# A decoder layer's RWKV recurrence spawned behind its key projection, with its low-rank factors loaded at the unit's start

## The chip, the cores and the metric

The kernel runs on one core of a Trainium2 chip. The metric is the time of one execution on the device in microseconds; the time before is the median of three runs. A profiled execution beside them gives the trace from which all rows below come.

## The reference, cut to what matters

One layer with 1024 tokens of width 2048, all in float32. One input projection feeds two groups of heads: 16 RWKV-7 heads of 64 and 16 sliding-window attention heads of 64. Both are gated, and one output projection adds their result to the input.

```python
z = rms_norm(x, norm_w) @ w_in                       # 2048 -> 6528 columns
# RWKV half: z = z + (z_prev - z) * mu; r, k, v, g, wl, al = split(z)
decay = exp(-exp(-softplus(-(w0 + tanh(wl) @ w2)) - 0.5))
a  = sigmoid(a0 + al @ a2)
kk = l2norm(k * k_k);  k = k * (1 + (a - 1) * k_a)
# per token and head:
sa = S @ -kk_t;  S = S * decay_t + sa (kk_t * a_t)^T + v_t k_t^T;  o_t = S @ r_t
o  = layernorm(o) * lnx_w + lnx_b + sum(r * k * r_k) * v;  y_rwkv = o * silu(g)
# attention half: window 128, sinks, relative bias, RMS norm of q and k
out = x + concat(y_rwkv, y_att) @ w_out
```

## The kernel before, in words

**Tiling.** The tokens are taken in two halves of 512 (`hf`), the heads in eight pairs (`p`). A *unit* is one pair in one half. A projection tile (`ztile`, L325) gives 128 columns of `z` for the 512 tokens: 16 blocks of the contraction, each with three matmuls of 128x512 (L346 and L347 for the high part of the weight with the high and low parts of the activation, L351 for the low part of the weight), so 48 matmuls. ScalarE cuts each weight piece into a high part (L321), GpSimd subtracts to get the low part (L322); SP's queue loads the pieces (L335).

**A unit** (`unit`, L802) makes six projection tiles in order: key, receptance, value and gate of the RWKV pair, then query and gate of an attention pair. `shifted` (L357) mixes each of the first four with the token before (L360 to L363). The first unit of the second half has two tiles more (`att_kv`).

**The recurrence of a pair** is `rwkv` (L830). `rwkv_prep` loads the low-rank factors (L376), splits them (L378 to L383), squares the key (L387), makes decay and mixing factors from two low-rank products (`lora`, L389) and a head-wise sum (`headsum`, L558), with a reciprocal on VectorE (L404), and writes the chunk factors Gt (L428, L429) and F (L433, L434). L443 multiplies these in two batches, L446 to L449 mask the products. `solve` (L462) inverts a triangular matrix per chunk of 64 tokens: blocks of 16 on VectorE (L470, L471), sent through DRAM by six DMAs (L476, L478) and put together by small matmuls (L486 to L521). Then `rwkv_chain` walks over the eight chunks, each step a matmul L587, copies L590 and L592, matmuls L594 and L595, and an update of the state on VectorE, L598. `rwkv_post` copies the outputs (L608), normalises them, transposes (L625) and writes to DRAM (L630). The attention of the pair is `att` (L669), with softmax on ScalarE and VectorE (L696 to L718).

**What sets the order.** The work is written as Python generators with due times on a clock of their own, `clk`, in units close to microseconds; a projection tile counts 15.36, a unit 92.16. `yield t` hands control back until the clock of the loop `run` (L100) reaches `t`, and sets the due time of what follows through `at` (L92); a generator that yields a time that is already past is continued at once, with that earlier due time. The framework below orders each engine's instructions by due time among those that can go. A buffer, though, is asked for where the Python code makes the tile, so in the order in which the generators are run: a tag has a fixed number of buffers (L79: four of `t`, five of `ta` and `zt`; three PSUM banks of `m`), and a later request waits behind an earlier one of its tag.

`rwkv` counts its due times from `t0`, the unit's start: the square is due at 15.5, the receptance's use at 32, L443 at 57.2 and 62.4, the solve from 65 to 88.5, the chain from 91.5, the post step at 135 to 154. Before the change it is spawned behind the value tile, at 46.1 (L808). The tag `t` serves the preparation (L386, L397, L402, L411, L416, L538, L548) and the post step (L604, L616, L626). At the start of the second half `hprep` (L273) loads 16 blocks of the input with SP's queue (L254), transposes them on TensorE (L287) and splits them.

Of the kernel before, what the change touches and what calls it, by code (L numbers as in the profile page):

```python
# [19 lines left out]
P = 128  # L20
# [3 lines left out]
T = 512  # L24
# [40 lines left out]
def layer(tc, x, norm_w, w_in, w_out, mu_rwkv, w0, w2, a0, a2, k_k, k_a, r_k, lnx_w, lnx_b,  # L65
          q_norm_w, k_norm_w, sinks, rel_bias, cst, out, groups=range(NP), do_out=True, dbg=None):
    nc = tc.nc
# [7 lines left out]
    def sb(shape, tag, bufs=1, dt=F32):  # L75
        return pool.tile(list(shape), dt, name=tag, tag=tag, bufs=bufs)
# [4 lines left out]
    def tmp(tag="t"):  # L81
        return sb([P, T], tag, NT.get(tag, 1))
# [6 lines left out]
    MM, TILE = 0.32, 48 * 0.32  # L89
    clk = [20]  # L90

    def at(t):  # L92
        tc.cur_priority = 100000 + int(t * 1000)
# [3 lines left out]
    def spawn(gen, t=None):  # L97
        heapq.heappush(live, (now[0] if t is None else t, next(order), gen))
# [268 lines left out]
    def v3(t, n=T):  # L367
        return t.rearrange("p (c t) -> p c t", c=NC)

    def rwkv_prep(t0, hf, p, S, lor, zk, zr, zv):  # L370
        cp = slice(p * P, (p + 1) * P)
        yield t0 + 0.262
        wr = sb([P, 2, P], "k1", 2)
        for i, w in enumerate((w2, a2)):
            for hr in HR:
                nc.sync.dma_start(wr[hr, i, :], w[0, :, cp])  # L376
        wla = sb([P, 2, P], "wla", 1, F32R)
        A.copy(wla[:], wr[:])  # L378
        for i, hr in enumerate(HR):
            A.copy(whz[hr, i, :], wr[hr, i, :])  # L380
        for i in range(2):
            hr = HR[1 - i]
            G.tensor_tensor(wla[hr, i, :], wr[hr, i, :], wla[hr, i, :].bitcast(F32), ALU.subtract)  # L383
        yield t0 + 15.5

        sq = tmp()  # L386
# [29 lines left out]
        kmul = tmp()  # L416
        A.activation(kmul[:], pa[:], AF.Identity, bias=dv["cka"][:, p:p + 1], scale=dv["hka"][:, p:p + 1])
        V.scalar_tensor_tensor(pa[:], pa[:], 1.0, n2[:], ALU.add, ALU.mult)
        k3, r3 = v3(zk[:, 0:T]), v3(zr[:, 0:T])
        kP = Pi  # L420
        V.tensor_tensor(kP[:], zk[:, 0:T], Pi[:], ALU.mult)
        yield t0 + 32
        Gt = sb([P, NC, P], "Gt")
        F = [sb([P, 2, 4, P], "F", 3) for _ in range(2)]
        for i, hr in enumerate(HR):
# [36 lines left out]
        def solve():  # L462
# [7 lines left out]
                V.tensor_tensor(q, Xs[:, 0:j, j:j + 1].to_broadcast([64, j, n]), X[:, j:j + 1, j + 1:16].to_broadcast([64, j, n]), ALU.mult)  # L470
                V.tensor_tensor(X[:, 0:j, j + 1:16], X[:, 0:j, j + 1:16], q, ALU.add)  # L471
            A.copy(Xs[:], X)

            q = nc.gpsimd if hf == 0 and p == groups[-1] else nc.sync
            for x, h in halves:
                q.dma_start(x5.rearrange("i b c s t -> (i b c) s t")[:, h, h], Xs[x])  # L476
            for i, b, r, cb in quads:
# [57 lines left out]
                A.copy(BE[hr, c0:c0 + 4, hr], b[hr, :, hr])  # L535
        spawn(solve())
        yield t0 + 69.5
        vb = tmp()  # L538
        V.transpose(vb[:], zv[:])
        v4 = vb[:].rearrange("p (c k v) -> p c k v", c=NC, k=2)  # L540
# [128 lines left out]
    def att(t0, hf, p, Q, sq, gz):  # L669
# [8 lines left out]
        rq = rsqrt(ms[:], 8, "q")  # L678
        bia = sb([P, 2, P], "bia")
        nc.sync.dma_start(bia[:], bass.AP(tensor=bd.tensor, offset=bd[p:p + 1, 0:1].offset, ap=[[P - 1, P], [8 * P * P, 2], [1, P]]))  # L680
        yield t0 + 108.5
        pts = []
        Ls = [tmp("ta")[:].rearrange("p (b k) -> p b k", b=NB) for _ in range(2)]
        for b2 in range(2):
# [117 lines left out]
    def unit(hf, p, h, lor):  # L802

        S = {}
        zk = yield from shifted(h, 8 + p)
        zr = yield from shifted(h, p)
        zv = yield from shifted(h, 16 + p, True)
        spawn(rwkv(clk[0] - 3 * TILE, hf, p, S, lor, zk, zr, zv))  # L808
        zg = yield from shifted(h, 24 + p)

        def gate():
            S["sil"] = silu2(zg[:])
            yield

        spawn(gate(), clk[0] + 15)
        if hf and p == groups[0]:
            yield from att_kv(hf, h)

        z = yield from ztile(h, RWKV_COLS + p * 64, RWKV_COLS + 512 + p * 64)
        Q, sq = sb([P, 2, T], "Q", 1, F32R), tmp("zt")  # L820
        for i, hr in enumerate(HR):
            A.copy(Q[hr, i, :], z[hr])
            V.tensor_tensor(Q[HR[1 - i], i, :], z[hr], Q[hr, i, :].bitcast(F32), ALU.subtract)
        A.activation(sq[:], z[:], AF.Square)
        z = yield from ztile(h, RWKV_COLS + 1280 + p * 64, RWKV_COLS + 1792 + p * 64)
        gz = tmp("zt")
        A.copy(gz[:], z[:])
        spawn(att(clk[0] - 6 * TILE, hf, p, Q, sq, gz))
# [58 lines left out]
```

## Time and profile before

| | |
|---|---|
| median of three runs | 2066.15 us (2063.0 to 2070.83) |
| profiled execution | 2064.07 us |
| its span in the trace | 2062.3 us |
| TensorE busy | 1980.4 us, 96% |
| VectorE, ScalarE, GpSimd busy | 1197.1, 1040.2, 860.0 us |
| mean granted TensorE clock | 0.986 of full speed |

Busy time is the union of an engine's instructions; TensorE's matmuls are pipelined and their ends modelled, so the starts of consecutive ones tell more than their durations. "Idle before" is the time in which an engine stood still ahead of an instruction, with what ended it. L numbers are lines of the kernel before.

### The profile page before, as it was taken

The numbers are of one execution on the slowest core, as the hardware profiler recorded it, in microseconds if no ns is written. First come the engines' busy times: TensorE is split into PE (matmuls) and PEld (weight loads), VectorE is DVE, ScalarE is ACT, GpSimd is POOL, SyncE is SP. The second block draws the span as 40 slices with busy tenths as digits, with TensorE's granted clock in tenths as the row PEclk, the third lists the DMA queues.
The fourth block names the chain that finished last, engine by engine and source line by source line (L and its number), as shares of the span: only waits on it lengthen the run. The fifth ranks groups of instructions, "written<-read, shape, count | busy, mean of one in ns | idle before, by whom it ended". The sixth has DMA issues, their size and how long they took to land.

```text
span 2062.3 us, 36490 instructions
## 1 busy us (share of the span) xinstructions
PE 1980.4 (96%) x13152; PEld 1599.5 (78%) x13152; DVE 1197.1 (58%) x2776; ACT 1040.2 (50%) x2563; POOL 860.0 (42%) x746
## 2 busy tenths in 40 slices
PE   7999999999999999799999999999999989999999
PEld 5777777777778787577777777777777778988887
DVE  5747585857575857585666676758585864011001
ACT  5445555555655555555656464655555563223221
POOL 4543434434343434245353434343443433444443
PEclk9999999999999999899999999999999999999999
DMA  7332323232333325223232323232323263455443
GB/s 175 90 93 62 94 64 87 70 83 73 82 76 82 79 74 137 63 70 93 69 98 64 90 61 92 58 98 64 87 68 84 72 182 120 150 159 168 137 134 118
DMA packets 410341, 197.01 MB, mean 96 GB/s; under 512 B 214893, under 2 KB 379088, under 8 KB 410160
## 3 DMA queue, kind: packets, MB, share of 16 engines
q1 hardware_dynamic: 369216, 181.70, 31.9%
q10 hardware_dynamic: 40000, 11.67, 2.4%
q0 software_dynamic: 944, 1.31, 0.5%
q8 instruction: 103, 1.69, 0.3%
q14 instruction: 78, 0.64, 0.1%
HBM read 173.51 MB, written 21.10 MB: 94 GB/s over the span
## 4 chain that ended last, share of the span: by engine, by line
PE 37%; DVE 9%; issue 3%; POOL 2%; ACT 1%; DMA 1%; SPq 0%; ACTq 0%; POOLq 0%; DVEq 0%
PE z L351 6%; PE z L346 6%; PE z L347 6%; PE z L789 2%; PE m L791 2%; PE z L790 2%; PE m L789 2%; PE z L791 2%; PE m L790 2%; POOL wl L322 1%; PE o L791 1%; PE o L789 1%; PE o L790 1%; DVE t L404 1%; PE o L587 1%
## 5 line engine op out<-in xcount | busy, mean ns | idle before, releaser
L322 POOL TENSOR_TENSOR wl<-wr,wh 128x512 fp32r<-128x512 f32 x536 | 704.8, 1319 | 1000.0 <-ACT wh L321 494.9
L346 PE MATMUL z<-hh,wh 128*128 128x512 f32 x1632 | 668.6, 410 | 2.4 <-ACT wh L321 1.7
L347 PE MATMUL z<-hl,wh 128*128 128x512 f32 x1632 | 656.0, 402 | 0.6 <-DVE hl L263 0.6
L321 ACT CAST wh<-wr 128x512 fp32r<-128x512 f32 x536 | 331.1, 619 | 530.6 <-PE z L347 170.4
L351 PE MATMUL z<-hh,wl 128*128 128x512 f32 x1632 | 482.5, 406 | 0.0
L346 PEld LDWEIGHTS z<-hh,wh 128*128 128x128 f32 x1632 | 311.9, 191 | 73.5 <-ACT wh L321 4.0
L347 PEld LDWEIGHTS z<-hl,wh 128*128 128x128 f32 x1632 | 312.1, 191 | 62.6 <-DVE hl L263 1.5
L351 PEld LDWEIGHTS z<-hh,wl 128*128 128x128 f32 x1632 | 299.7, 190 | 63.8 <-issue 3.6
L354 DVE TENSOR_TENSOR z<-z,R 128x512 f32<-128x512 f32 x102 | 70.9, 695 | 117.9 <-PE z L351 115.4
L789 PE MATMUL z<-wh,hh 128*128 128x256 f32 (+1 forms) x352 | 112.1, 319 | 9.6 <-ACT hh L259 5.9
L590 ACT ACTIVATE s<-svu,pe 64x64 f32<-64x64 f32 x256 | 88.1, 344 | 52.0 <-DVE svu L598 48.6
L791 PE MATMUL z<-wh,hl 128*128 128x256 f32 (+1 forms) x352 | 111.1, 316 | 0.0
L790 PE MATMUL z<-wl,hh 128*128 128x256 f32 (+1 forms) x352 | 111.0, 315 | 0.0
L587 PEld LDWEIGHTS o<-svu,F 128*128 128x128 f32 x512 | 81.3, 190 | 27.4 <-DVE svu L598 16.8
L470 DVE TENSOR_TENSOR pr<-X,ch 64x14 f32<-64x14 f32 (+6 forms) x224 | 42.2, 188 | 98.3 <-ACT ch L465 91.4
L587 PE MATMUL o<-svu,F 128*128 128x64 f32 x512 | 83.9, 264 | 7.8 <-DVE svu L598 7.3
L797 DVE TENSOR_TENSOR ta<-z,ta 128x256 f32<-128x256 f32 (+1 forms) x22 | 9.9, 492 | 128.8 <-PE z L791 128.8
L598 DVE SCALAR_TENSOR_TENSOR svu<-ch,pe,s 64x64 f32<-64x64 f32 x224 | 63.1, 282 | 28.6 <-PE ch L594 23.8
L789 PEld LDWEIGHTS z<-wh,hh 128*128 128x128 f32 x352 | 67.0, 191 | 15.0 <-ACT hh L259 6.3
L797 DVE TENSOR_TENSOR ta<-m,ta 128x512 f32<-128x512 f32 x9 | 6.1, 690 | 124.8 <-PE m L791 124.8
L790 PEld LDWEIGHTS z<-wl,hh 128*128 128x128 f32 x352 | 67.1, 191 | 4.3
L791 PEld LDWEIGHTS z<-wh,hl 128*128 128x128 f32 x352 | 67.0, 190 | 4.3
(278 smaller groups left out, 3343.6 us busy)
## 6 DMA issues: line engine op xcount, KB each, us to landing
wr<-in_w_in SPq DMA_DIRECT2D x280, 256.0 KB, 2.9
wr<-in_w_in SPq DMA_DIRECT2D x256, 128.0 KB, 2.6
wr<-in_w_out SPq DMA_DIRECT2D x64, 256.0 KB, 2.9
wr<-in_w_out SPq DMA_DIRECT2D x128, 128.0 KB, 2.9
ta<-in_x SPq DMA_DIRECT2D x37, 256.0 KB, 5.2
zt<-yd SPq DMA_DIRECT2D x32, 256.0 KB, 3.5
out<-ta SPq DMA_DIRECT2D x24, 256.0 KB, 4.1
yd<-ta ACTq DMA_DIRECT2D x16, 256.0 KB, 2.6
```

Of the source, the lines that this page charges most:

```text
L321: A.copy(hi[:], raw)
L322: G.tensor_tensor(lo[:], raw, hi[:].bitcast(F32), ALU.subtract)
L346: PE.matmul(z[:], lhsT=wh, rhs=hh[kk][:], start=(kk == 0), stop=False)
L347: PE.matmul(z[:], lhsT=wh, rhs=hl[kk][:], start=False, stop=False)
L351: PE.matmul(z[:], lhsT=lo[:, k * P:(k + 1) * P], rhs=hh[kk][:], start=False, stop=(kk == KT - 1))
L354: V.tensor_tensor(z[:], z[:], R[:], ALU.mult)
L587: PE.matmul(O[:, c, i, :], lhsT=F[c // 4][:, i, c % 4, :], rhs=svu[:, i, c, :], start=c % 4 == 0 and i == 0, stop=False, skip_group_check= ...
L590: A.activation(s0[hr], svu[hr, i, c, :], AF.Copy, scale=pe[hr, c:c + 1])
L598: V.scalar_tensor_tensor(dst, ch[hr, i, :], pe[hr, c:c + 1], s0[hr], ALU.mult, ALU.add)
L789: PE.matmul(o, lhsT=yh[k][:, ts], rhs=wh, start=k == 0 and tt % n == 0, stop=False, skip_group_check=True)
L790: PE.matmul(o, lhsT=yh[k][:, ts], rhs=wl, start=False, stop=False, skip_group_check=True)
L791: PE.matmul(o, lhsT=yl[k][:, ts], rhs=wh, start=False, stop=k == KT - 1 and tt % n == n - 1, skip_group_check=True)
```

## The change

Five edits: the low-rank factors are loaded and split by a function of their own, called at the unit's start and due 8 before it (DMAs) and 2 behind it (splits), in a buffer of tag `t` where it was one of `k1`; `rwkv` is spawned behind the key tile, and gets the list in which receptance and value are put later; `rwkv_prep` takes them from the list where it uses them; the last pair's solve in the first half sends its six DMAs by SP's queue where it was GpSimd's; the attention asks for its logits buffers at 103.2 where it was 108.5.

```diff
--- before.py
+++ after.py
@@ -367,20 +367,27 @@
     def v3(t, n=T):
         return t.rearrange("p (c t) -> p c t", c=NC)
 
-    def rwkv_prep(t0, hf, p, S, lor, zk, zr, zv):
+    def low_rank(t0, p):
+
         cp = slice(p * P, (p + 1) * P)
-        yield t0 + 0.262
-        wr = sb([P, 2, P], "k1", 2)
+        at(t0 - 8)
+        wr = tmp()[:, 0:2 * P].rearrange("p (i c) -> p i c", i=2)
         for i, w in enumerate((w2, a2)):
             for hr in HR:
                 nc.sync.dma_start(wr[hr, i, :], w[0, :, cp])
+        at(t0 + 2)
         wla = sb([P, 2, P], "wla", 1, F32R)
-        A.copy(wla[:], wr[:])
+        A.copy(wla[:], wr)
         for i, hr in enumerate(HR):
             A.copy(whz[hr, i, :], wr[hr, i, :])
         for i in range(2):
             hr = HR[1 - i]
             G.tensor_tensor(wla[hr, i, :], wr[hr, i, :], wla[hr, i, :].bitcast(F32), ALU.subtract)
+        return wla
+
+    def rwkv_prep(t0, hf, p, S, lor, wla, zs):
+
+        zk = zs[0]
         yield t0 + 15.5
 
         sq = tmp()
@@ -416,10 +423,12 @@
         kmul = tmp()
         A.activation(kmul[:], pa[:], AF.Identity, bias=dv["cka"][:, p:p + 1], scale=dv["hka"][:, p:p + 1])
         V.scalar_tensor_tensor(pa[:], pa[:], 1.0, n2[:], ALU.add, ALU.mult)
-        k3, r3 = v3(zk[:, 0:T]), v3(zr[:, 0:T])
+        k3 = v3(zk[:, 0:T])
         kP = Pi
         V.tensor_tensor(kP[:], zk[:, 0:T], Pi[:], ALU.mult)
         yield t0 + 32
+        zr = zs[1]
+        r3 = v3(zr[:, 0:T])
         Gt = sb([P, NC, P], "Gt")
         F = [sb([P, 2, 4, P], "F", 3) for _ in range(2)]
         for i, hr in enumerate(HR):
@@ -470,8 +479,7 @@
                 V.tensor_tensor(q, Xs[:, 0:j, j:j + 1].to_broadcast([64, j, n]), X[:, j:j + 1, j + 1:16].to_broadcast([64, j, n]), ALU.mult)
                 V.tensor_tensor(X[:, 0:j, j + 1:16], X[:, 0:j, j + 1:16], q, ALU.add)
             A.copy(Xs[:], X)
-
-            q = nc.gpsimd if hf == 0 and p == groups[-1] else nc.sync
+            q = nc.sync
             for x, h in halves:
                 q.dma_start(x5.rearrange("i b c s t -> (i b c) s t")[:, h, h], Xs[x])
             for i, b, r, cb in quads:
@@ -535,6 +543,7 @@
                 A.copy(BE[hr, c0:c0 + 4, hr], b[hr, :, hr])
         spawn(solve())
         yield t0 + 69.5
+        zv = zs[2]
         vb = tmp()
         V.transpose(vb[:], zv[:])
         v4 = vb[:].rearrange("p (c k v) -> p c k v", c=NC, k=2)
@@ -678,7 +687,7 @@
         rq = rsqrt(ms[:], 8, "q")
         bia = sb([P, 2, P], "bia")
         nc.sync.dma_start(bia[:], bass.AP(tensor=bd.tensor, offset=bd[p:p + 1, 0:1].offset, ap=[[P - 1, P], [8 * P * P, 2], [1, P]]))
-        yield t0 + 108.5
+        yield t0 + 103.2
         pts = []
         Ls = [tmp("ta")[:].rearrange("p (b k) -> p b k", b=NB) for _ in range(2)]
         for b2 in range(2):
@@ -802,10 +811,11 @@
     def unit(hf, p, h, lor):
 
         S = {}
-        zk = yield from shifted(h, 8 + p)
-        zr = yield from shifted(h, p)
-        zv = yield from shifted(h, 16 + p, True)
-        spawn(rwkv(clk[0] - 3 * TILE, hf, p, S, lor, zk, zr, zv))
+        wla = low_rank(clk[0], p)
+        zs = [(yield from shifted(h, 8 + p))]
+        spawn(rwkv(clk[0] - TILE, hf, p, S, lor, wla, zs))
+        zs.append((yield from shifted(h, p)))
+        zs.append((yield from shifted(h, 16 + p, True)))
         zg = yield from shifted(h, 24 + p)
 
         def gate():
```

## Rows read from the trace of the kernel before

**Rows 1.** Page part 1: busy time of the engines over the span

```profile
PE 1980.4 (96%) x13152; PEld 1599.5 (78%) x13152; DVE 1197.1 (58%) x2776; ACT 1040.2 (50%) x2563; POOL 860.0 (42%) x746
```

**Rows 2.** Stretches: length, busy PE, PEld, DVE, ACT, POOL, clock, DMA share, GB/s

```profile
351.00:448.00 97.00, 94.58 (x667) 75.09 (x666) 65.47 (x160) 54.30 (x142) 39.70 (x35) 0.98 0.31 78
...
1515.00:1612.00 97.00, 94.51 (x674) 75.71 (x673) 66.28 (x158) 54.84 (x142) 39.94 (x35) 0.98 0.31 78
...
724.70:846.20 121.50, 105.87 (x888) 84.51 (x887) 69.78 (x168) 59.35 (x156) 45.29 (x42) 0.90 0.36 97
1177.90:1275.60 97.70, 95.25 (x677) 76.31 (x676) 66.76 (x158) 54.60 (x143) 39.96 (x35) 0.98 0.31 78
```

**Rows 3.** Timeline, TensorE, one unit: start, us, instruction, [idle before <-releaser]

```profile
1177.85 0.39 PE L346 MATMUL z<-hh,wh 128*128 128x512 f32 x1
1178.08 0.39 PE L347 MATMUL z<-hl,wh 128*128 128x512 f32 x1
...
1243.05 0.48 PE L443 MATMUL m<-F,Gt 64*128 64x128 f32 x2 [0.98 <-DVE F L434]
1243.99 1.17 PE L443 MATMUL m<-F,Gt 64*128 64x128 f32 x14 [0.46 <-DVE F L434]
...
1245.69 0.63 PE L346 MATMUL z<-hh,wh 128*128 128x512 f32 x1
...
1248.25 0.45 PE L346 MATMUL z<-hh,wh 128*128 128x512 f32 x1
```

**Rows 4.** Timeline, VectorE, the same unit

```profile
1194.89 0.75 DVE L361 SCALAR_TENSOR_TENSOR zt<-z,par,zt 128x511 f32<-128x511 f32 x1 [0.76 <-ACT zt L360]
...
1234.10 3.33 DVE L404 RECIPROCAL t<-t 128x512 f32<-128x512 f32 x1
...
1243.43 0.42 DVE L434 TENSOR_TENSOR F<-zt,Pc 64x256 f32<-64x256 f32 x1
```

**Rows 5.** Timeline, ScalarE, the same unit

```profile
1222.76 1.50 ACT L608 COPY t<-o 64x256 f32<-64x256 f32 x4
...
1226.96 0.71 ACT L387 ACTIVATE t<-zt,par 128x512 f32<-128x512 f32 x1
```

**Rows 6.** Timeline, TensorE, end of the first half

```profile
797.83 1.16 PE L443 MATMUL m<-F,Gt 64*128 64x128 f32 x16
...
822.40 0.71 PE L351 MATMUL z<-hh,wl 128*128 128x512 f32 x2
833.77 1.07 PE L486 MATMUL m<-k,Eab 32*32 32x32 f32 x64 [10.66 <-DVE k L482]
...
844.34 1.06 PE L287 MATMUL m<-cst,ta 128*128 128x128 f32 x4
...
846.17 0.50 PE L346 MATMUL z<-hh,wh 128*128 128x512 f32 x1
```

**Rows 7.** Waits: engine line <- releaser: us in total, times, longest

```profile
POOL wla L383 <- ACT wla L378: 57.4, 15, 15.7
...
PE m L443 <- DVE F L434: 18.9, 26, 1.0
...
PE o L587 <- DVE svu L598: 7.3, 14, 1.4
...
PE m L532 <- DVE F L449: 2.9, 7, 0.4
```

**Rows 8.** Timeline, solve's copy and return: ScalarE and VectorE, two units

```profile
822.89 0.36 ACT L472 COPY X<-ch 64x256 f32<-64x256 f32 x1
...
833.17 0.45 DVE L482 STREAM_TRANSPOSE k<-dg 128x256 f32<-128x256 f32 x1 [9.33 <-DMA dg<-xd]
...
1273.52 0.37 ACT L472 COPY X<-ch 64x256 f32<-64x256 f32 x1 [1.17 <-DVE ch L471]
...
1281.96 0.45 DVE L482 STREAM_TRANSPOSE k<-dg 128x256 f32<-128x256 f32 x1 [3.40 <-DMA dg<-xd]
```

**Rows 9.** Line L376, SP: issues, ns min/median/max, first and last start

```profile
L376 SPq DMA_DIRECT2D k<-in_w x32: 471/532/1524, 24.6 to 1583.9; - x32
L376 SPq DMA_DIRECT2D k<-in_a x32: 587/595/1702, 27.8 to 1585.2; - x32
```

**Rows 10.** Timeline, TensorE, the chain beside softmax in another unit

```profile
1304.61 0.43 PE L587 MATMUL o<-svu,F 128*128 128x64 f32 x2 [0.56 <-DVE svu L598]
```

## The prediction

> **What bounds the kernel now.** I read the page first: TensorE is busy for 1980.4 of 2062.3 us [rows 1]. That is an upper figure, because modelled matmul ends overlap, so I then read stretches of one unit (one head pair in one half). A usual unit lasts 97 to 98 us; in 1177.9 to 1275.6 TensorE is busy for 95 us, VectorE for 67, ScalarE for 55, GpSimd for 40 [rows 2]. Nothing but TensorE is full, so a unit gets shorter only where TensorE waits or runs slowly. TensorE takes its instructions in a fixed order: one matmul that waits holds the projections behind it.
>
> Then the timeline of such a unit. Its key tile starts on TensorE at 1177.85 [rows 3]. The key projection is ready in SBUF at about 1195.6, when the mixing step L361 ends [rows 4]. But the first step of the recurrence, the square at L387, runs only at 1226.96, 31 us later, on the heels of the copies L608 of the unit before (1222.76) [rows 5]. No data links the two. What links them is the tag `t`: the old order of the Python code asks for the post step's buffers (due 135 of the unit before, which is 42.8 of this one) ahead of the preparation's (due 15.5), since `rwkv` is spawned only behind the value tile (46.1). So the preparation stands behind a post step that is due 27 later.
>
> The late preparation then runs as one burst on VectorE: the reciprocal L404 at 1234.10, the last factor L434 that the first batch of L443 needs at 1243.43 [rows 4]. TensorE comes to L443 before that and waits 0.98 us and 0.46 us [rows 3]. [...]
>
> Last, the end of the first half: the unit there lasts 121.5 us at a mean clock of 0.90 [rows 2]. Projections run out at about 823.1, and TensorE sits idle for 10.66 us until L486 at 833.77, the solve of the last pair [rows 6]. The transposes L287 of the second half follow only at 844.34 [rows 6].
>
> **The change part by part.** The clock of the code runs 92.2 per unit, the chip 97: due times stretch by 1.05.
>
> (1) `rwkv` is spawned behind the key tile. No computing is added or removed; the preparation's requests for `t` and for the PSUM tag `m` move ahead of the post step's. The square can then start at 1195.6 instead of 1227, and the factors F are limited by the receptance tile (due 30.7, so about 34 us into the unit) and by VectorE's other work. From the unit's 34th us to L443's due time (57.2, so 60 us, 1238) there are 26 us, where the work from the reciprocal to the last needed factor now takes 9.8 us of VectorE (1234.10 to 1243.85, [rows 4]). So L443 finds its operands ready.
>
> Gain a: the waits of L443 for F, 18.9 us in 26 waits, that is 13 units [rows 7]. Gain b: the waits of L532 behind it, 2.9 us in 7 [rows 7]. Gain c: the slow stretches. Six of the seventeen 97 us stretches stand at 0.98 (the first and last in rows 2, outside the boundary); one costs 6 x (0.43 - 0.23) = 1.2 us, together 7.
>
> (2) At the boundary the second batch of L443 ran at 797.83, 73 us into its unit [rows 6]; with its operands ready it comes at its due time of 62.4, 65.5 us in, or 790.2. From there to L486 it took 35.9 us [rows 6], so L486 would be ready at 826.1. (3) That unit's solve moves its six DMAs from GpSimd's queue to SP's. On GpSimd's it took 10.3 us from the copy L472 (822.89) to L482 (833.17); a unit on SP's took 8.4 (1273.52 to 1281.96) [rows 8]. That is 1.9 more: ready at about 824.2, and the idle time falls from 10.7 to about 1. Gain d: 9.5 us. What would take it away: SP is also carrying the second half's input blocks then, and a DMA that waits there for its buffer holds all behind it. Bounds for the boundary: nothing, and the whole 23 us from 823.1 to the second half's first projection at 846.17 [rows 6]. I stay near the low middle, since the transposes' PSUM banks are still asked for behind the solve's.
>
> (4) The low-rank factors go into a `t` buffer at 8 before the unit, not a `k1` one. The same four DMAs stand in SP's queue, at medians of 0.53 and 0.60 us two each, 2.3 us a unit [rows 9]. They pass weight loads that are issued 17 ahead of use, which is the cover; without it each unit would lose up to 2.3 us, 37 in all. They hold a fourth of tag `t` for about 10 units of clock in which the post step due before is done and the preparation is not begun. The splits L378 to L383 move with them: GpSimd stands still at L383 for 57.4 us in 15 waits today, with its weight splits queued behind [rows 7], and no projection waits for that, so ending it earns nothing. I take 0. (5) The attention's logits buffers are asked for at 103.2, not 108.5, ahead of the preparation's first banks: no instruction differs; 0, with bounds of a few tenths either way that the terms below contain.
>
> (6) What is late next. The chain of the unit before (91.5 to 131, so 0 to 41 us into this unit) and the attention's softmax now share VectorE with the preparation. A chain step's update L598 that becomes ready behind the reciprocal waits up to 3.3 us (1234.10, [rows 4]), and TensorE waits at L587. Lower bound: a gain of 7.3, if the chain's dates, 5 apart, are kept so well that L587's present waits go [rows 7]. Upper bound: 3.3 us once a unit, 53, and a slow stretch behind each, 16 x 1.2 = 19. The nearest row is today's: chain beside softmax, L587 waits 0.56 us [rows 10]. I take that once more a unit, 9 us.
>
> [...]
>
> Sum: 18.9 + 2.9 + 7 + 9.5 - 9 = 29 us. The profiled execution took 2064.07 us, 1.8 beyond its span and 0.1% under the median of 2066.15; 2064 - 29 = 2035 by the one, 2037 by the other. I say 2036.
>
> **The rivals.** *The wait moves to the chain (slower).* Place: L587 and L594 on TensorE, behind L598 on VectorE. For it: in the first 41 us of a unit VectorE would hold chain, softmax, projection endings and the preparation at once, and the reciprocal alone lasts 3.33 us [rows 4]. Against: a unit leaves VectorE 31 us to spare [rows 2], and post step and factors have slack to slip behind the chain. Price: 53 + 19 = 72 lost against 38 gained, 2064 + 34 = 2098. It decides from 3.0 us a unit (38 + 10 over 16); below that it only eats the gain.
>
> *The wait keeps its size.* VectorE gets no further with F by L443 than now, or the chain takes as much as L443 gives back (1.8 us a unit). Only the boundary's 9.5 remains: about 2055, at the edge of what counts as faster. For it: the burst's work is the same, and the softmax stands in its way. Against: 31 us of head start.
>
> *It does not do what it says.* Something else than `t` holds L387, such as the bank order of `m`, and the square stays behind the post step: 2064. For it: the trace shows L387 behind L608 [rows 5], not why; it cannot tell a buffer from sheer order. Against: an operand that lies ready for 31 us, and ScalarE at only 55 of 98 us [rows 2].
>
> **How the numbers follow.** The forecast has 0.64, the wait that keeps its size 0.15, no effect 0.06, the slower rival 0.15. A measurement of this kernel tells about 0.5%, 10 us, from no change. Faster than that: the forecast and a fair part of the second case at its edge, less the forecast's own weak end: 0.66. Same: 0.19. Slower: 0.15. The forecast's own range is 2012 (no new wait, and the whole 23 us of the boundary: 2064 - 28.8 - 23) to 2053 (nothing at the boundary, and new waits twice as large: 2064 - 28.8 + 18). The range that should hold 8 in 10 goes from 2010 to 2072, which takes in the case with no effect and the mild part of the slower one.
>
> **What would show each step.** Right: in the changed kernel's timelines the square stands about 18 us after its unit's first key matmul, ahead of the post step's copies; "PE m L443 <- DVE F" is gone from the list of waits or under 4 us; no 0.98 in the stretches; L486 at the boundary waits under 3 us; the units last about 95. Wrong: the square still 49 us in; the wait of L443 unchanged; L587 or L594 with more than 1 us a unit; SP waiting ahead of the solve's DMAs at the boundary; or projections that wait for `wh` or `wl`, ScalarE's and GpSimd's splits come late behind the moved work.

## The result, and the profile after

The changed kernel takes 2038.06 us (median of 4 runs, 2035.18 to 2040.28), the kernel before, run beside it, 2065.92 (2063.0 to 2070.83): a ratio of 0.9862, 95% interval 0.9839 to 0.9885. The forecast was 2036. Line numbers from here on are those of the changed kernel: the square is L394 (was L387), the reciprocal L411 (L404), F L442 and L443 (L433, L434), the batches of L443 are now L452, the solve's first products L494 (L486), the chain's matmuls L596, L603, L604 (L587, L594, L595) and its update L607 (L598). Two single edits of the kernel before have numbers of their own, given where they are quoted.

The page, part 1, of the changed kernel, against [rows 1]:

```profile
span 2033.4 us, 36474 instructions
...
PE 1956.4 (96%) x13152; PEld 1588.8 (78%) x13152; DVE 1154.3 (57%) x2776; ACT 1038.9 (51%) x2563; POOL 855.4 (42%) x740
```

The span is 28.9 us shorter, TensorE's busy time 24.0. VectorE's fell by 42.8 with the same 2776 instructions, which no step of the prediction speaks of: added one by one, their durations are 31 us less, so some instructions got shorter. That is the first hint of what the experiments found.

The waits, against [rows 7] (us in total, times, longest):

```profile
PEld o L596 <- DVE svu L607: 30.9, 44, 2.5
...
PE o L596 <- DVE svu L607: 14.1, 19, 2.1
```

Among all of TensorE's waits none of L452 for F is left, where 18.9 us stood, and none of the transposes behind it (2.9). The chain's wait has doubled, from 7.3 us in 14 to 14.1 in 19. In all kernels of this document with the late spawn it is 4.7 to 7.3 us; in all with the early spawn and GpSimd's subtractions whole it is 14.1 to 28.7.

One unit, the pair that [rows 3 to 5] show, in the changed kernel: ScalarE, then VectorE, then TensorE (start, us, instruction). The unit's first key matmul is at 1162.9.

```profile
1180.88 0.73 ACT L394 ACTIVATE t<-zt,par 128x512 f32<-128x512 f32 x1
...
1210.96 1.50 ACT L617 COPY t<-o 64x256 f32<-64x256 f32 x4
```
```profile
1196.92 3.35 DVE L411 RECIPROCAL t<-t 128x512 f32<-128x512 f32 x1
...
1209.86 0.41 DVE L443 TENSOR_TENSOR F<-zt,Pc 64x256 f32<-64x256 f32 x1
```
```profile
1227.93 1.16 PE L452 MATMUL m<-F,Gt 64*128 64x128 f32 x16
...
1233.60 1.16 PE L452 MATMUL m<-F,Gt 64*128 64x128 f32 x16
1234.69 0.51 PE L346 MATMUL z<-hh,wh 128*128 128x512 f32 x1
```

The square stands 18.0 us into the unit (49 before) and 30 ahead of the post step's copies, where it used to follow them. The reciprocal is at 34.0 instead of 56. The factors are ready 15 us before L452, which runs without a bracket, that is without idle time before it.

Where the time went: the span cut at the first key matmul of units, in us. "End of half 1" is the last unit there with the first tile of half 2.

| stretch | before | after | difference |
|---|---|---|---|
| to the first key matmul, and the first unit | 140.6 | 141.5 | +0.9 |
| six usual units of half 1 | 584.1 | 563.2 | -20.9 |
| end of half 1 | 143.3 | 136.2 | -7.1 |
| first two units of half 2 | 210.6 | 225.7 | +15.1 |
| five usual units of half 2 | 490.3 | 473.7 | -16.6 |
| last unit and output projection | 493.3 | 493.2 | -0.1 |

So the usual units gained 37.5 us and the end of half 1 7.1, and the first two units of half 2 gave 15.1 back. Stretches (length, busy PE, PEld, DVE, ACT, POOL, clock, DMA share, GB/s) of the two units in the changed kernel, a usual unit, and the last of half 1:

```profile
840.90:971.20 130.30, 122.61 (x799) 96.84 (x799) 85.81 (x193) 71.25 (x176) 53.24 (x44) 0.99 0.28 73
971.20:1066.50 95.30, 88.29 (x436) 70.24 (x435) 62.54 (x141) 46.18 (x116) 40.95 (x35) 0.95 0.30 78
...
1162.90:1257.50 94.60, 92.86 (x678) 74.57 (x677) 63.65 (x158) 55.05 (x143) 40.05 (x35) 1.00 0.32 81
...
704.80:818.60 113.80, 102.65 (x887) 82.87 (x885) 65.64 (x168) 58.16 (x151) 40.74 (x34) 0.93 0.40 102
```

and of the same two in the kernel before:

```profile
868.10:994.90 126.80, 122.28 (x799) 95.94 (x799) 86.31 (x193) 71.41 (x176) 53.18 (x44) 1.00 0.29 76
994.90:1078.70 83.80, 83.73 (x436) 67.17 (x435) 59.35 (x141) 45.34 (x113) 39.73 (x33) 1.00 0.33 87
```

The second of them, with 436 matmuls where a usual unit has 678, was full: 83.73 of 83.80 us. Now it has 7 us of idle TensorE and a clock of 0.95. The usual unit shown no longer has 0.98, but 1.00.

### The profile page after: what moved, and what is told of

The parts are those of the page before. It is cut to its first block, busy times and chain, and to the rows that moved or that the text cites. A ratio compares the mean times of both kernels' runs of the same rounds, so it can differ in the third digit from the quotient of the medians.

```text
span 2033.4 us, 36474 instructions
## 1 busy us (share of the span) xinstructions
PE 1956.4 (96%) x13152; PEld 1588.8 (78%) x13152; DVE 1154.3 (57%) x2776; ACT 1038.9 (51%) x2563; POOL 855.4 (42%) x740
## 4 chain that ended last, share of the span: by engine, by line
PE 40%; DVE 8%; issue 3%; POOL 1%; ACT 1%; DMA 1%; ACTq 0%; SPq 0%; POOLq 0%; DVEq 0%
PE z L351 6%; PE z L346 6%; PE z L347 6%; PE z L798 2%; PE z L800 2%; PE z L799 2%; PE m L800 2%; PE m L798 2%; PE m L799 2%; POOL wl L322 1%; DVE ta L714 1%; PE o L800 1%; PE o L798 1%; PE o L799 1%; DVE t L411 1%
## 5 line engine op out<-in xcount | busy, mean ns | idle before, releaser
L322 POOL TENSOR_TENSOR wl<-wr,wh 128x512 fp32r<-128x512 f32 x536 | 704.4, 1318 | 952.2 <-ACT wh L321 506.7
L346 PE MATMUL z<-hh,wh 128*128 128x512 f32 x1632 | 661.4, 405 | 3.5 <-ACT hh L262 2.3
L351 PE MATMUL z<-hh,wl 128*128 128x512 f32 x1632 | 483.8, 406 | 0.0
L351 PEld LDWEIGHTS z<-hh,wl 128*128 128x128 f32 x1632 | 301.0, 190 | 65.1 <-issue 2.7
L596 PEld LDWEIGHTS o<-svu,F 128*128 128x128 f32 x512 | 81.5, 189 | 38.8 <-DVE svu L607 30.9
L596 PE MATMUL o<-svu,F 128*128 128x64 f32 x512 | 85.9, 264 | 15.0 <-DVE svu L607 14.1
L798 PEld LDWEIGHTS z<-wh,hh 128*128 128x128 f32 x352 | 67.1, 191 | 15.1 <-ACT hh L259 6.8
L607 DVE SCALAR_TENSOR_TENSOR svu<-ch,pe,s 64x64 f32<-64x64 f32 x224 | 62.9, 281 | 17.3 <-PE ch L603 11.1
```

Source lines behind the costliest of these rows:

```text
L322: G.tensor_tensor(lo[:], raw, hi[:].bitcast(F32), ALU.subtract)
L346: PE.matmul(z[:], lhsT=wh, rhs=hh[kk][:], start=(kk == 0), stop=False)
L351: PE.matmul(z[:], lhsT=lo[:, k * P:(k + 1) * P], rhs=hh[kk][:], start=False, stop=(kk == KT - 1))
L596: PE.matmul(O[:, c, i, :], lhsT=F[c // 4][:, i, c % 4, :], rhs=svu[:, i, c, :], start=c % 4 == 0 and i == 0, stop=False, skip_group_check= ...
L607: V.scalar_tensor_tensor(dst, ch[hr, i, :], pe[hr, c:c + 1], s0[hr], ALU.mult, ALU.add)
L798: PE.matmul(o, lhsT=yh[k][:, ts], rhs=wh, start=k == 0 and tt % n == 0, stop=False, skip_group_check=True)
```

## The experiments

Each is compared with the kernel before, run on the same chip. In the stretches, one profile differs from another by up to some 3 us where the kernels are alike: with GpSimd's queue restored for one pair (below), the six units that lie ahead of that pair, and which the edit doesn't touch, came out at 566.5 against 563.2. The chain's wait differs more: 14.1 us in the changed kernel, 15.4 to 21.3 in the four kernels below whose edits leave the chain alone (the queue, the late post step, the transposes, and the last two together).

**The early spawn alone.** The kernel before with `rwkv` spawned behind the key tile, and nothing else.

```diff
...
-        zk = yield from shifted(h, 8 + p)
-        zr = yield from shifted(h, p)
-        zv = yield from shifted(h, 16 + p, True)
-        spawn(rwkv(clk[0] - 3 * TILE, hf, p, S, lor, zk, zr, zv))
+        zs = [(yield from shifted(h, 8 + p))]
+        spawn(rwkv(clk[0] - TILE, hf, p, S, lor, zs))
+        zs.append((yield from shifted(h, p)))
+        zs.append((yield from shifted(h, 16 + p, True)))
```

> The kernel before with one edit: the recurrence is spawned behind its key tile; factors, queue and logits stay as they were. Theory (the order in which buffers are asked for carries the change): the waits of the factor matmuls L443 for F, 18.9 us before, fall under 3 us, a usual unit lasts 93 to 95 us, and the time is 2036 to 2046. Rival (the factors loaded ahead carry it): the preparation still starts late, the waits stay at 15 us or more, and the time is 2058 to 2070.

Measured: 2049.96 us, ratio 0.993 (0.9906 to 0.9955), 4 us above the range that was expected, though L443's wait is gone from the list and the square is at 18.0. The chain's wait is three times that of [rows 7]; in this kernel the chain is L591 and L602:

```profile
PE o L591 <- DVE svu L602: 23.3, 30, 1.9
```

The usual units take 569.6 and 478.4 us in the two halves (six and five of them), and the first two units of half 2 227.2. This edit alone thus brings most of the gain in the usual units and the whole loss.

**Everything but the early spawn.** The changed kernel with `rwkv` spawned behind the value tile again.

```diff
-        spawn(rwkv(clk[0] - TILE, hf, p, S, lor, wla, zs))
         zs.append((yield from shifted(h, p)))
         zs.append((yield from shifted(h, 16 + p, True)))
+        spawn(rwkv(clk[0] - 3 * TILE, hf, p, S, lor, wla, zs))
```

> The kernel after with the spawn put back behind the value tile; the factors are loaded ahead, SP's queue and the logits at 103.2 are kept. Theory (order of requests): the square runs again about 49 us into its unit, the waits for F return to 15 to 20 us, and the time is 2056 to 2070. Rival (factors ahead): the time stays at 2034 to 2045.

Measured: 2060.76 us, 0.9978 (0.9965 to 0.999). The square is back at 48.6 to 49.3, and so is the wait:

```profile
PE m L452 <- DVE F L443: 18.8, 26, 1.0
```

The first two units of half 2 take 210.1, as before the change. So the order of spawning removes the wait and makes the loss; the other edits are worth some 5 us by themselves, and 12 beside the early spawn (2049.96 to 2038.06). The early factors, the queue and the logits at 103.2 were not separated further, but for the queue.

**GpSimd's queue for the last pair's solve.** The changed kernel with the old choice of queue.

```diff
-            q = nc.sync
+            q = nc.gpsimd if hf == 0 and p == groups[-1] else nc.sync
```

> The kernel after, with the last pair's solve of the first half on GpSimd's queue again. Theory (the queue is worth the 1.4 to 1.9 us that the way from the copy to the transpose is shorter on SP's): the idle time before L494 grows from 8.1 to 9 to 11 us and the time by 0 to 4 us. Rival (SP's queue holds the solve behind the input blocks, so the move cost something): the idle time falls below 8 us and the time by 1 us or more.

Measured: 2041.41 us, 0.9887 (0.9865 to 0.9908). L494 waits 10.4 us at the end of half 1 where the changed kernel's waits 8.1. The sign and the size fit; against the changed kernel's 2038.06 the 3.3 us are within the intervals. The chain's wait shows how far it moves without an edit of its own:

```profile
PE o L596 <- DVE svu L607: 21.3, 29, 2.1
```

**Which buffer held the preparation.** The kernel before, its spawn unchanged, with the post step's three buffers in a tag of their own (two of a new tag, `t` and `wr` one fewer each; one input block of the second half moves to the new tag).

```diff
-    NT = dict(t=4, ta=5, zt=5, wr=4, wh=3, wl=3)
+    NT = dict(t=3, tq=2, ta=5, zt=5, wr=3, wh=3, wl=3)
...
-        on = tmp()
+        on = tmp("tq")
...
-        sq = tmp()
+        sq = tmp("tq")
...
-        y = tmp()
+        y = tmp("tq")
```

> The kernel before with its late spawn, but the post step's three buffers have a tag of their own (two buffers; t has three, and the raw weights wr three instead of four to make room; one input block of the second half takes the new tag). Theory (tag t alone holds the preparation behind the post step): the square runs ahead of the post step's copies, near 18 us into its unit, and the waits for F fall under 6 us. Rival (the PSUM banks of m, asked for in the same order, hold it too): the square itself runs early, but the low-rank products and all behind them stay near 50 us, and the waits for F stay at 12 us or more. The time depends on the third raw weight buffer as well and decides nothing.

Measured: 2043.08 us, 0.9893 (0.9864 to 0.9921). ScalarE and VectorE in the unit that starts at 1167 (lines of the kernel before):

```profile
1185.25 0.73 ACT L387 ACTIVATE t<-zt,par 128x512 f32<-128x512 f32 x1
...
1211.90 1.50 ACT L608 COPY tq<-o 64x256 f32<-64x256 f32 x4
```
```profile
1221.76 3.33 DVE L404 RECIPROCAL t<-t 128x512 f32<-128x512 f32 x1
```

With `t` free the square runs 18 us in, but the low-rank products stay at 51 and the reciprocal at 54.6, behind the post step on VectorE. So `t` held the square alone. The products' factors are split by 1188.2, and TensorE runs them only at 1218.28, right behind the attention's first L734 (1217.91), whose bank of the PSUM tag `m` the code asks for just ahead of theirs. So `m`, the place that the third rival named, is the likely holder of the rest, and behind the attention rather than the post step; this is read from the order of the requests and these times, and no run gave `m` more banks. The early spawn moves the requests of all tags. And yet most of L443's 18.9 us [rows 7] is gone here too (waits of this kernel):

```profile
PE m L443 <- DVE F L434: 3.2, 7, 0.5
...
PE m L443 <- DVE F L449: 2.8, 13, 0.2
```

The burst ended only 0.4 to 1.8 us earlier in the unit, and that was enough for two thirds: the wait was short and stood at the edge. The first two units of half 2 take 211.5: no loss.

**The reciprocal left out**, in the kernel before and in the changed one.

```diff
-        V.reciprocal(n2[:], n2[:])
+        V.tensor_scalar(n2[:], n2[:], 0.0, 1e-7, ALU.mult, ALU.add)
```

> The kernel before with the same op left out. Theory (TensorE's wait for F is the end of one VectorE burst, of which the reciprocal is a third): the burst ends 2.6 us sooner, the waits of L443 fall from 18.9 to under 8 us, the slow stretches go with them, and the time falls by 12 to 25 us. Rival (L443 is placed where F is reckoned ready, so a shorter burst moves both): the waits stay at 14 us or more and the time falls by less than 8.

> The kernel after with the reciprocal L411 (3.33 us on VectorE) left out: a multiply-add that yields a constant, about 0.7 us, stands in its place, so the key normalisation is not computed. Theory (the chain's updates stand behind the reciprocal now, as the slower rival of the prediction had it in small): the waits of the chain's L596 for L607, 14.1 us in 19 on the matmuls, fall under 7 us, and the time falls by 10 to 25 us to 2013 to 2028. Rival (they stand behind softmax and projections as before): the waits stay at 11 us or more and the time falls by less than 6.

Measured: in the kernel before, 2044.4 us, 0.9904 (0.9886 to 0.9922); in the changed one, 2052.19 us, 0.9944 (0.9926 to 0.9962). The kernel before gained 20 us, as expected, though more of L443's wait is left than was said, now mostly for the mask L449 (1.3 us before):

```profile
PE m L443 <- DVE F L449: 8.4, 14, 1.7
PE m L443 <- DVE F L434: 3.2, 7, 0.5
```

Its first two units of half 2 take 215.8 us, 5.2 more than before. The changed kernel lost 14 us. Its chain's wait without its longest VectorE instruction:

```profile
PE o L596 <- DVE svu L607: 28.7, 30, 2.2
```

The idea that the chain's wait comes from the reciprocal fell: with it gone, the wait is longer than in any kernel that has it. Most late L607 follow a short instruction that took too long: shortly ahead of 16 of the 19 in the changed kernel stands a VectorE instruction that lasted over 0.2 us more than its like. Around one of them (VectorE, then GpSimd):

```profile
1101.30 3.35 DVE L411 RECIPROCAL t<-t 128x512 f32<-128x512 f32 x1
1104.56 0.90 DVE L724 TENSOR_TENSOR sm<-sm,es 128x4 f32<-128x4 f32 x1
1105.38 0.27 DVE L607 SCALAR_TENSOR_TENSOR svu<-ch,pe,s 64x64 f32<-64x64 f32 x1
```
```profile
1102.94 2.50 POOL L322 TENSOR_TENSOR wl<-wr,wh 128x512 fp32r<-128x512 f32 x2 [5.81 <-ACT wh L321]
```

L724 adds four columns, took 0.15 us at 1099.46, and here lasts until 1105.46, when GpSimd's two weight subtractions end at 1105.44. The view of single lines of the changed kernel gives durations in ns (min/median/max):

```profile
L724 DVE TENSOR_TENSOR sm<-sm,es x32: 98/152/1185, 174.0 to 1677.1; 128x4 f32<-128x4 f32 x32
...
L727 DVE TENSOR_SCALAR ta<-ta,sm x128: 269/281/1316, 174.3 to 1679.2; 128x128 f32<-128x128 f32 x128
...
L607 DVE SCALAR_TENSOR_TENSOR svu<-ch,pe,s x224: 258/284/292, 159.2 to 1684.8; 64x64 f32<-64x64 f32 x112
```

L724 and L727 read SBUF only, and stretch to four and more times their median, by up to 1.04 us, where a subtraction lasts 1.3. L607 reads PSUM (`ch`), and none of 224 passes 292 ns. In the kernel without the reciprocal the same makes the loss of half 1. In six of its units L607 comes behind four L727, two of them held beside GpSimd by 1.0 us each, and TensorE waits 2.15 to 2.18 us. Five of these are usual units; the six usual units of half 1 lose 13.3 us together. One of them (VectorE, GpSimd, TensorE):

```profile
274.52 2.92 DVE L727 TENSOR_SCALAR ta<-ta,sm 128x128 f32<-128x128 f32 x4
```
```profile
274.60 1.36 POOL L322 TENSOR_TENSOR wl<-wr,wh 128x512 fp32r<-128x512 f32 x1 [0.37 <-ACT wh L321]
276.10 1.26 POOL L437 TENSOR_TENSOR Gt<-t 64x512 f32<-64x512 f32 x1
```
```profile
278.20 0.66 PE L596 MATMUL o<-svu,F 128*128 128x64 f32 x2 [2.17 <-DVE svu L607]
```

The next two experiments test whether GpSimd is the cause.

**No subtraction on GpSimd.** The changed kernel without L322; L351 takes the high part of the weight in place of the low part, which changes the values of all projections, and the high parts get the low parts' three buffers.

```diff
-    NT = dict(t=4, ta=5, zt=5, wr=4, wh=3, wl=3)
+    NT = dict(t=4, ta=5, zt=5, wr=4, wh=6, wl=3)
...
-        hi, lo = sb([P, 512], "wh", NT["wh"], F32R), sb([P, 512], "wl", NT["wl"], F32R)
+        hi = sb([P, 512], "wh", NT["wh"], F32R)
...
-        G.tensor_tensor(lo[:], raw, hi[:].bitcast(F32), ALU.subtract)
-        return hi, lo
+        return hi, hi
```

> The kernel after with GpSimd's subtraction L322 left out: the matmuls of the low weight parts take the high parts again, as many and as long as before, so the low parts of the weights are missing from the result (the room of their buffers goes to the high parts). Theory (VectorE instructions with two inputs in SBUF stand still while a GpSimd instruction runs; the fixed order of TensorE was laid out without that, and its waits at the chain and the factors are the difference): L724 and its like keep to their short times (0.15 us, none over 0.6), VectorE's time above its own short forms falls from 98 us to under 40, the waits of the chain's L596 on the matmuls fall from 14.1 to under 6 us, and the time falls by 10 to 30 us. Rival (the long L724 has another cause, and the chain waits for sheer VectorE work): the waits stay at 10 us or more, the time within 8 us of the kernel after.

Measured: 1994.17 us, 0.9668 (0.9654 to 0.9683), 44 us under the changed kernel and so more than the 10 to 30 that were expected. Page, line of the sum (L723 here) and the chain's wait (L595 and L606 here):

```profile
PE 1946.7 (98%) x13152; PEld 1579.1 (79%) x13152; DVE 1089.2 (55%) x2776; ACT 1038.9 (52%) x2563; POOL 157.3 (8%) x204
...
L723 DVE TENSOR_TENSOR sm<-sm,es x32: 92/148/161, 163.7 to 1638.0; 128x4 f32<-128x4 f32 x32
```
```profile
PE o L595 <- DVE svu L606: 6.8, 12, 0.8
```

VectorE does the same 2776 instructions in 65.1 us less (1154.3 - 1089.2), and the longest of the sums falls from 1185 ns to 161. The chain's wait is back where the late spawn has it, a little above the 6 that were expected. The first two units of half 2 take 205.9 us, not 225.7: 19.8 of the 39.3 us of span lie there. The usual units of half 2 gain 5.3, those of half 1 nothing (564.2 for 563.2). Of the rest, 8.8 lie in the first row of the table and 5.0 in the last, where weights that need no subtraction also come sooner, so those cannot be put down to VectorE.

**The subtraction in two halves.** The changed kernel, nothing left out.

```diff
-        G.tensor_tensor(lo[:], raw, hi[:].bitcast(F32), ALU.subtract)
+        for s in (slice(0, 256), slice(256, 512)):
+            G.tensor_tensor(lo[:, s], raw[:, s], hi[:, s].bitcast(F32), ALU.subtract)
```

> The kernel after with GpSimd's subtraction of each weight piece in two instructions of 256 columns. Theory (as long as one GpSimd instruction runs, so long VectorE stands): a blocked VectorE instruction waits at most about 0.7 us instead of 1.3, the chain's waits fall from 14.1 to 6 to 11 us, and the time falls by 3 to 12 us. Rival (GpSimd's back-to-back halves hold VectorE just as long, or the second instruction's own cost delays the weights): the chain's waits stay at 12 us or more, and the time stays within 3 us or grows.

Measured: 2026.82 us, 0.9825 (0.981 to 0.9839), 11 us under the changed kernel, though GpSimd is busy for 942.1 us where it was 855.4. What fell is the single stall more than their sum. Beside the halves no VectorE instruction is held for more than 0.78 us, beside the whole subtractions for up to 1.9; but 175 are held here for over 0.2 us where 134 were, and VectorE's held time is 87 us for 96 (counted as in the last section). The sum (L725 here) and the chain's wait:

```profile
L725 DVE TENSOR_TENSOR sm<-sm,es x32: 99/151/499, 172.5 to 1669.8; 128x4 f32<-128x4 f32 x32
```
```profile
PE o L597 <- DVE svu L608: 8.7, 19, 1.6
```

**A later post step at the start of half 2.** The first unit there has two tiles more, so a solve and half a chain that a usual unit leaves to the next are done within it, and the second unit has 436 matmuls. The first unit's post step, due 135 from its own start, is due 12 into the second unit, not 43 as usual; there it meets softmax and the early preparation. VectorE, GpSimd and TensorE of the changed kernel in that unit:

```profile
1016.89 1.43 DVE L442 SCALAR_TENSOR_TENSOR F<-zt,nkk,Pc 64x256 f32<-64x256 f32 x1
1018.24 1.52 DVE L443 TENSOR_TENSOR F<-zt,Pc 64x256 f32<-64x256 f32 x1
1019.77 0.47 DVE L442 SCALAR_TENSOR_TENSOR F<-zt,nkk,Pc 64x256 f32<-64x256 f32 x1
...
1021.45 0.69 DVE L734 TENSOR_TENSOR ta<-m,cst 128x512 f32<-128x512 f32 x1
```
```profile
1016.47 3.00 POOL L322 TENSOR_TENSOR wl<-wr,wh 128x512 fp32r<-128x512 f32 x2 [2.02 <-ACT wh L321]
```
```profile
1011.91 0.75 PE L731 MATMUL m<-cst,ta 128*128 128x128 f32 x4 [2.48 <-ACT t L636]
...
1022.20 0.43 PE L743 MATMUL m<-ta,vt 128*64 128x128 f32 x2 [2.25 <-DVE ta L734]
1023.52 0.48 PE L743 MATMUL m<-ta,vt 128*64 128x128 f32 x1 [0.89 <-DVE ta L734]
```

Two factors take 1.43 and 1.52 us instead of 0.47 and 0.42 while GpSimd subtracts, the attention's L734 stands behind them in VectorE's queue, and TensorE waits 2.25 us for it. The wait of L731 has another cause, the post step's L636. The longest wait of the two units is in the first of them, where the post step of the last pair of half 1 comes late on VectorE:

```profile
895.74 0.63 PE L634 MATMUL m<-cst,t 128*128 128x128 f32 x4 [3.11 <-DVE t L630]
```

The edit moves the post step of the first unit, and not that one, by two tiles:

```diff
+        if hf and p == groups[0]:
+            t0 += 2 * TILE
         yield t0 + 135
```

> The kernel after, with the post step of the first unit of the second half due two tiles (30.7) later. Theory (the second unit of that half lasts 95.3 us where it lasted 83.8, since that post step, due two tiles early against its neighbours, now meets softmax and preparation on VectorE): the waits of L731 and L743 there go, the two first units of the half take 212 to 218 us instead of 225.7, and the time falls by 7 to 14 us to 2024 to 2031. Rival (softmax and preparation collide there whatever the post step does): the two units stay above 222 us and the time within 4 us of the kernel after.

Measured: 2031.71 us, 0.9846 (0.9827 to 0.9865), an interval that overlaps the changed kernel's. L731's wait is gone, and the two units take 222.0 us, 3.7 less: the larger gain that was hoped for did not come, since the attention's L743 (L745 in this kernel) still waits 4.5 us and the late post step of half 1 3.1. Of the 8.0 us between the two profiles another 3.3 lie in the first row of the table, ahead of all that the edit touches.

**The transposes of the second half in another PSUM tag.** The prediction left them behind the solve's banks.

```diff
-                b = ps("m")
+                b = ps("z" if hf and q < 2 else "m")
```

> The kernel after, with the first eight of the sixteen transposed blocks of the second half put into PSUM banks of z, not m. Theory (the transposes L287 stand behind the solve's last banks of m, and TensorE idles meanwhile): L287 starts before L494 of the last pair, the stretch from that unit's start to the first unit of the second half, 136.2 us, shrinks by 3 to 9 us, and the time with it. Rival (the input blocks or VectorE's splits hold the transposes, or the solve's end holds the half's first projections anyway): the stretch stays within 2 us.

Measured: 2028.63 us, 0.9828 (0.981 to 0.9846), and the end of half 1 takes 130.4 us, 5.8 under the changed kernel's. L494's wait is gone; the transposes wait there instead, 3.8 us in three waits for VectorE's splits (L263) and 1.7 us for other things.

**Both together**, and then **all three** with the halves. In the second expectation below, the transposes meant are those of the second half's input blocks, L287, and the subtractions are GpSimd's L322:

> The kernel after with both edits of the two runs before: the late post step of the second half's first unit, and eight transposed blocks in banks of z. Each alone gave 6 to 9 us in different stretches. If they are independent the time is 2020 to 2027; if the orders that TensorE is given shift against each other it is 2028 to 2035.

> The change with three further edits together: the post step of the first unit of the second half later, the transposes of the key in a PSUM tag of another name, and VectorE's long subtractions in two halves. If the three act in different stretches (the two first gave 2025.2 together, the halves alone 2026.8, from 2038.1), their gains add to some 2010 to 2020 us. Rival: what one gains is lost where the other has shifted the order of the requests or of VectorE's queue, and the time stays at 2022 to 2030.

Measured: 2025.16 us, 0.9818 (0.9801 to 0.9835), and 2016.57 us, 0.9757 (0.9743 to 0.977). With the halves the usual units of half 2 take 469.9 us, the first two 219.2, the end of half 1 130.1. This is the fastest version that computes everything, 49.7 us under the kernel before and 21.5 under the change.

## Why the prediction was right, and where it was not

**The total was right by terms that missed in both directions.** The sum was 29 us and the span fell by 28.9. But for the usual units the steps gave 18.9 + 2.9 + 7 - 9 = 19.8, and they gained 37.5; the first two units of half 2 then lost 15.1 that no step and no rival had. That the sum came out to the microsecond is luck; that the wait of L443 goes with the early spawn is not. The terms, one by one:

- *Gains a and b*, the waits of L443 and L532, 21.8 us: gone, as said. Counted from start to start on TensorE (each gap less that line's usual one, its lower quartile) they were worth 27.2 + 4.0 = 31.2 before and less than 0.7 apiece after: the term was 9.4 us too small. Of that, 1.3 are L443's listed waits for L449, which the prediction left out. For the rest, the list gives idle time only, and consecutive matmuls overlap in the trace (0.39 us long, 0.23 from start to start [rows 3]), which is lost across an idle time; that this is all of it was not shown.
- *Gain c*, the slow stretches: the usual units ran for 20.5 us at a granted clock of 0.50 before and for none after. The term's six matmuls at 0.43 us, against 0.23 [rows 3], are those from 1245.69 to 1248.25, where the granted clock is 0.50; from 1177.85 to 1185 it is 1.00. About half of the 20.5, 10 us, is an estimate of the gain, from 0.43 us a matmul against 0.23; it is a little more than the 7. The kernel as a whole gave up less, 59.6 us at 0.50 before and 48.3 after: 13.7 us came up in the first two units of half 2, which had none, behind the waits shown above.
- *Gain d*, 9.5 us at the end of half 1: 7.1 came, for another reason. L494's wait fell only from 10.66 to 8.09 us [rows 6], not to 1. L494 is indeed 7.7 us earlier in its unit (101.4 us in, 109.1 before), most of the 9.5; but TensorE's projections also ran out 5 us earlier in the unit (93.3 against 98.4), so the idle time moved with it. A wait between two ends that both move is not shortened by what the later end gains. The solve's return took 8.9 us on SP (796.51 to 805.42) for 10.3 on GpSimd's queue [rows 8], 1.4 for the predicted 1.9. Of the input blocks on SP, which the prediction named as what would take the gain away, one (L254) waited 19.0 us for its buffer, and SP issued nothing from 804.06 to 823.08; but the last of the solve's DMAs had been issued by 803.57.

```profile
797.20 0.71 PE L351 MATMUL z<-hh,wl 128*128 128x512 f32 x2
806.01 1.08 PE L494 MATMUL m<-k,Eab 32*32 32x32 f32 x64 [8.09 <-DVE k L490]
```

- *Step (4)*, the factors loaded ahead, at 0: too low, by some 5 us with the other small edits, as the run with the late spawn shows.
- *Step (6)*, the chain, 9 us: from start to start the chain's first matmul lost 9.0 before and 18.3 after, 9.3 more. The size fits in this profile, with some luck, since the listed wait moves from 14.1 to 21.3 us between kernels that leave the chain alone. The mechanism was not right. The prediction made the reciprocal the obstacle; leaving it out made the wait longer. A chain update does stand behind the reciprocal (above, L607 at 1105.38 behind L724 and the 3.35 us of L411), but most of the added wait comes from short instructions that last longer beside GpSimd's: without the subtraction the listed wait is 6.8 us. VectorE was held so in the kernel before too, and for longer, 128 us against 96; the early preparation moved it to where the chain and softmax stand behind it.
- *The cause of the late square*, the tag `t`: right for the square, wrong for the rest of the burst, which stood, as far as the run tells, behind the PSUM tag `m`. It cost nothing, since the spawn moves both, but someone who had only given the post step its own `t` would have found the reciprocal where it was. That this run gains some 22 us all the same, with the burst at most 1.8 us earlier, says that the wait and its slow stretches hung on very little; that its third raw weight buffer less has no part in it was not tried.

**The rivals.** The chain did take some of the gain, some 0.6 us a unit, far from the 3.0 from which the slower rival would decide. The wait did not keep its size, and the change does what it says.

**The step that was left out** is the start of half 2. The prediction took all units as usual ones, but the first of half 2 has two tiles more, and its post step comes two tiles early against the second. There the earlier preparation meets softmax and post step, and VectorE is busy for 28.9 of the 30 us from 991 to 1021. The second unit loses 11.5 of the 15.1 us, the first 3.5, of which the late L634 is 3.1. That the loss hangs on GpSimd is shown by leaving its subtraction out: the two units fall to 205.9 us, below the 210.6 before the change, of which TensorE was idle for only 4.6, so that the subtraction can have cost little there. And none of TensorE's listed waits in the two units of the changed kernel is for a weight.

**What stays open.** The changed kernel's loss of 14 us without the reciprocal is in the chain's wait (18.3 to 33.2 us from start to start), and VectorE's instructions are held longer in all (113.6 us over their own usual durations against 97.7). In half 1 the waits of 2.2 us shown above make most of it; why the shorter work falls more often on GpSimd's was not followed further. Nor was the kernel before tried without GpSimd's subtraction. Which of the small edits brings the 12 us beside the early spawn was not tried one by one.

## What to carry to other kernels

Where buffers are handed out in the order in which generators are run, spawn work by its due time, and look in the changed trace for the work that now meets it, above all in the units that are shorter than the rest. Read the maximum beside the median of a short instruction: a 0.15 us sum that once takes 1.2 says that something else holds the engine, and no sum of medians shows it. Where VectorE is on the path, try cutting long GpSimd instructions on SBUF into shorter ones even if that costs GpSimd time: here 87 us more of it gave 11 us of the whole.

## What the runs showed of the hardware

In these kernels VectorE instructions with two SBUF operands, and some others such as the scaling L727, mostly lasted longer when begun beside a GpSimd instruction (of 180 sums, products and the like without an operand in PSUM, begun so in the changed kernel, 108 by over 0.2 us): the sum L724, over four columns and with a median of 0.15 us, took up to 1185 ns beside subtractions of 1.3 us, up to 499 beside ones of about half the length (0.74), and at most 161 without them. Those with an operand in PSUM did not: L607 never passed 293 ns, 107 of its 256 begun beside a GpSimd instruction. This holds in all fourteen kernels, when each VectorE instruction is set against the usual duration of its line and shape (the lower quartile, the least over the kernels). Every one that lasted over 0.2 us more overlaps a GpSimd instruction, and none of the 1493 in each kernel with an operand in PSUM lasted over 0.03 us more. Together the long ones hold VectorE for 128 us before the change, 96 after it, 87 with the halves and 32 without the weights' subtraction, which by the busy time too is worth 65; and the chain and softmax stand behind them on VectorE: the chain's listed wait is 14.1 us after the change and 6.8 without the subtraction.

Second, waits of TensorE that the list gives as 18.9, 1.3 and 2.9 us were worth some 31, before the stretches behind them at a granted clock of 0.50 are counted, 20.5 us in the usual units.
